# Strassen's seven products in place of eight for the down projection of an MLP, with weight sums by accumulating fetches and activation sums on GpSimd

## The chip, the cores and the metric

The kernel runs on one core of a Trainium2 chip. The metric is the device time of one execution in microseconds (us), lower is better. A core has TensorE (matmuls, PE in the profile; PEld is its weight load), VectorE (DVE), ScalarE (ACT), GpSimd (POOL) and SyncE (SP, which here only issues transfers). Matmul results land in the banks of PSUM; all other tiles lie in SBUF.

## The reference

The kernel computes one layer of a decoder trunk in fp32: three token mixers, their merge, and an MLP. The change touches the last product of the MLP alone, with x of 512 tokens x 1024 channels and 3072 hidden channels:

```python
h2 = rms_norm(x, norm_ffn[l])
up = causal_dwconv(h2 @ w_up[l], ffn_conv_w[l], ffn_conv_b[l])
gate_h, val_h = jnp.split(up, 2, axis=-1)
x = x + (jax.nn.gelu(gate_h, approximate=True) * val_h) @ w_down[l]
...
return rms_norm(x, final_norm)
```

## The kernel before, in words

**Products of three matmuls.** Every fp32 operand of a product is kept as a head and a rest. `split` (L94, L95) makes the head by a copy on ScalarE into the matmul's own type and the rest by a subtraction on VectorE. `mm3` (L101) then issues three matmuls for one product: head by head, head by rest, rest by head. All big matmuls have a 128x128 stationary and a 128x512 moving operand.

**Units.** The program is a list of units, each with a block of weights (512 KB), and of steps of other work between them. `emit` walks the list and calls `fetch` (L152: one load on SyncE's queue and the splits) for a unit two units ahead of it (`AHEAD`). The order in which each engine gets its instructions follows from that list and from a scheduler behind it.

**The MLP.** Hidden channels come in three groups of 1024 (eight tiles of 128). For a group, 16 up units run first: 24 matmuls each, one 128x512 result [hidden channel, token]. `up_evac` reads it with one ACT operation (L910) and two DVE operations (L912, the causal convolution). After each second unit `up_done` applies GELU on ScalarE, multiplies on VectorE (L923) and splits the product into head and rest, so that it can be the stationary operand of the down projection.

**The down projection** of a group adds [512 tokens, 1024 hidden] by [1024, 1024] weights to the residual `x2`: eight tiles [128 tokens, 512 channels] `x2[t][c]`, called `m` in the profile. `down_units` makes two rounds of four units, one round for each half c of the output channels. A unit of `token_units` holds 256 hidden rows of weights and has 24 matmuls, six into each of four PSUM banks (one for each 128 tokens t); behind the fourth unit the four banks are added to x2 by DVE (`evac`, L858). So a group has 8 x 24 = 192 matmuls. In the last group the second round is made by `token_held`: all four blocks of weights are held, and the tiles of tokens follow one another with 24 matmuls each, so that the final norm of one runs beside the matmuls of the next.

**The final norm** of 128 tokens: `evac` squares x2 with a sum along the rows (ACT, L121); `final` multiplies the second half by the gain on GpSimd (L951), takes the sum of both squares (L872), runs `rsqrt` (L109 to L115, twelve small DVE operations that each need the one before), scales the first half (`normed`, L877, DVE) and the second (L954, ACT), and stores both (L955, L956).

The name `raw` stands for weights as loaded, `whi` and `wlo` for head and rest of a block, `r` for heads and rests in smaller tiles, `f` for fp32 tiles, `mm` for PSUM banks, `st` for columns of row statistics.

## Time and profile before

| | |
|---|---|
| time, median of 3 runs | 954.41 us (954.19 to 954.55) |
| span of the profiled execution | 952.6 us, granted TensorE clock 0.997 |
| median less span | 1.8 us |
| TensorE busy | 940.8 us (99%), 4522 matmuls |
| VectorE, ScalarE, GpSimd busy | 572.4, 452.8, 11.1 us |
| the three groups of the MLP | from 559.54 us to the last matmul at 943.84 us |

One execution was recorded by the profiler. Its span runs from its first to its last instruction, and the runs' median is 1.8 us above it. In the views below, a row of the timeline has start, duration, engine, line, operation, the tile written and the tiles read, the shape, and in brackets the idle time before it and what ended that. Where a row stands for several instructions (x2, x3), its duration is from the first one's start to the last one's end. Neighbours in a row overlap a little, so the time that one more of them takes is the difference between rows of different counts.

### The profile page before, as it was taken

Reading aid. Unit: us, or ns where it says so; the run is one execution under the profiler, and the core shown is the slowest. Engines: PE = TensorE matmul, PEld = TensorE weight load, DVE = VectorE, ACT = ScalarE, POOL = GpSimd, SP = SyncE. Lnnn points to the kernel's source line nnn. Section 1 sums busy time; section 2 is a strip of 40 time slices with the busy share of each in tenths; the row PEclk is TensorE's granted clock in tenths of the full one; section 3 lists DMA queues with packets and bytes.
Section 4 is the critical chain, followed back from the end, with each engine's and each line's share of the span. In section 5 each row is a group of like instructions: output and inputs, shape, how many; then the busy total and the mean of one; then the engine's idle time right before and its main releaser. Section 6 shows DMA issues by size and latency. Waiting matters only on the chain.

```text
span 952.6 us, 11687 instructions
## 1 busy us (share of the span) xinstructions
PE 940.8 (99%) x4522; PEld 798.2 (84%) x4522; DVE 572.4 (60%) x1003; ACT 452.8 (48%) x682; POOL 11.1 (1%) x27
## 2 busy tenths in 40 slices
PE   8999999999999999999999999999999999999996
PEld 6899888887897789998888898888888888888885
DVE  7897754565744774485576756663456643556646
ACT  7565645684955783343334434442244432344432
POOL 0000000000000000000000000000000000000002
PEclk9999999999999999999999999999999999999998
DMA  7446212222232232222266202232232332322312
GB/s 231 152 138 193 67 57 68 80 92 78 75 117 79 77 99 84 78 94 72 67 197 224 77 23 88 89 105 95 90 109 89 97 102 90 107 93 91 131 45 88
DMA packets 30839, 95.95 MB, mean 101 GB/s; under 512 B 3568, under 2 KB 4736, under 8 KB 30784
## 3 DMA queue, kind: packets, MB, share of 16 engines
q1 hardware_dynamic: 30208, 94.16, 30.7%
q10 hardware_dynamic: 576, 1.05, 0.3%
q8 instruction: 35, 0.57, 0.2%
q14 instruction: 20, 0.16, 0.1%
HBM read 93.10 MB, written 2.10 MB: 100 GB/s over the span
## 4 chain that ended last, share of the span: by engine, by line
PE 95%; DVE 3%; DMA 0%; ACT 0%; issue 0%; SPq 0%; DVEq 0%; ACTq 0%
PE mm L101 89%; PE sm L101 3%; PE mm L328 1%; DVE wlo L95 1%; PE sm L787 1%; DMA m<-in_xT 0%; DVE r L95 0%; PE sm L789 0%; PE sm L773 0%; DVE m L296 0%; PE sm L760 0%; PE sm L895 0%; PE sm L808 0%; DVE hl L95 0%; PE sm L502 0%
## 5 line engine op out<-in xcount | busy, mean ns | idle before, releaser
L95 DVE TENSOR_TENSOR wlo<-raw,whi 128x1024 fp32r<-128x1024 f32 (+3 forms) x171 | 189.2, 1110 | 215.7 <-PE mm L101 98.6
L94 ACT ACTIVATE whi<-raw 128x1024 fp32r<-128x1024 f32 (+3 forms) x171 | 164.6, 966 | 198.1 <-PE mm L101 176.4
L101 PE MATMUL mm<-h2l,whi 128*128 128x512 f32 x360 | 140.1, 389 | 0.0
L101 PE MATMUL mm<-h2h,whi 128*128 128x512 f32 x360 | 139.9, 389 | 0.0
L101 PE MATMUL mm<-whi,r 128*128 128x512 f32 (+1 forms) x448 | 135.3, 381 | 0.0
L101 PE MATMUL mm<-hh,whi 128*128 128x512 f32 x288 | 113.9, 396 | 0.0
L101 PE MATMUL mm<-hl,whi 128*128 128x512 f32 x288 | 112.6, 391 | 0.0
L101 PE MATMUL mm<-r,whi 128*128 128x512 f32 (+1 forms) x448 | 98.3, 368 | 0.0
L101 PEld LDWEIGHTS mm<-whi,r 128*128 128x128 f32 x448 | 83.7, 188 | 15.0
L101 PEld LDWEIGHTS mm<-r,whi 128*128 128x128 f32 x448 | 77.9, 189 | 14.6 <-issue 0.8
L101 PE MATMUL mm<-h2h,wlo 128*128 128x512 f32 x360 | 88.9, 389 | 0.0
L101 PE MATMUL mm<-wlo,r 128*128 128x512 f32 (+1 forms) x224 | 85.6, 382 | 0.2 <-DVE wlo L95 0.2
L101 PEld LDWEIGHTS mm<-h2l,whi 128*128 128x128 f32 x360 | 67.6, 188 | 14.0
L101 PEld LDWEIGHTS mm<-h2h,wlo 128*128 128x128 f32 x360 | 67.6, 188 | 14.0
L101 PEld LDWEIGHTS mm<-h2h,whi 128*128 128x128 f32 x360 | 67.5, 188 | 13.9
L912 DVE SCALAR_TENSOR_TENSOR f<-mm,prm,f 128x511 f32<-128x511 f32 x96 | 71.7, 746 | 7.8 <-ACT f L910 6.1
L101 PE MATMUL mm<-hh,wlo 128*128 128x512 f32 x288 | 71.2, 389 | 0.0
L101 PEld LDWEIGHTS mm<-hh,whi 128*128 128x128 f32 x288 | 54.1, 188 | 11.6 <-issue 0.4
L101 PEld LDWEIGHTS mm<-hh,wlo 128*128 128x128 f32 x288 | 54.1, 188 | 11.2
L101 PEld LDWEIGHTS mm<-hl,whi 128*128 128x128 f32 x288 | 54.1, 188 | 10.7
L94 ACT ACTIVATE r<-f 128x512 fp32r<-128x512 f32 (+4 forms) x47 | 27.2, 589 | 65.0 <-DVE f L923 61.8
L101 PE MATMUL mm<-r,r 128*128 128x512 f32 (+1 forms) x240 | 56.8, 391 | 0.0
(191 smaller groups left out, 1208.0 us busy)
## 6 DMA issues: line engine op xcount, KB each, us to landing
raw<-in_wup SPq DMA_DIRECT2D x48, 512.0 KB, 3.5
raw<-in_wch SPq DMA_DIRECT2D x40, 512.0 KB, 3.3
raw<-in_wdown SPq DMA_DIRECT2D x24, 512.0 KB, 3.5
raw<-in_wbr SPq DMA_DIRECT2D x24, 384.0 KB, 3.1
raw<-in_wvg SPq DMA_DIRECT2D x12, 384.0 KB, 3.0
raw<-in_wout SPq DMA_DIRECT2D x8, 512.0 KB, 3.5
raw<-in_wmk SPq DMA_DIRECT2D x6, 512.0 KB, 3.4
raw<-in_wmv SPq DMA_DIRECT2D x8, 384.0 KB, 3.1
```

Of the source, the lines that this page charges most:

```text
L94: nc.scalar.activation(hi, src, AF.Copy)
L95: (eng or nc.vector).tensor_tensor(out=lo, in0=src, in1=hi.bitcast(F32), op=ALU.subtract)
L101: nc.tensor.matmul(ps, lhsT=l, rhs=r, start=first and i == 0, stop=last and i == len(seq) - 1)
L328: nc.tensor.matmul(ps[u], lhsT=a, rhs=b, start=q == 0 and i in (0, 2), stop=q == KD - 2 and i >= len(seq) - 2)
L787: nc.tensor.matmul(ps[:, j, :], lhsT=sT[h][:, t, :], rhs=vt[t][hp][:, j, :], start=True, stop=t == 0)
L912: nc.vector.scalar_tensor_tensor(out=a[:, j:], in0=ps[:, :S - j], scalar=col(C_FCW + 48 * (2 - j) + f), in1=a[:, j:], op0=ALU.mult, op1=AL ...
```

## The change

The product of a group is made from halves of both operands: the tokens in two halves of 256, the hidden channels in two halves (even and odd tiles), the output channels in two halves of 512. The plain way has eight products of such halves. The change uses seven, called a1, a2, c1, b1, c2, b2 and b3, on sums and differences of the halves (Strassen's scheme in Winograd's form). Each product has two parts p (four of the hidden tiles' pairs each half) of 12 matmuls, so a group has 14 units of 12 = 168 matmuls.

What goes with it:

- Weights. A product's weights are half tiles of 128x512. B11, B21, B22 and B12 are loaded plainly by SyncE's queue (L994). The sums of weights are made in place: a fetch from GpSimd's queue adds another quarter of the weights to what lies in SBUF (`accum_op`, L999): B11 + B12, then + B22, then + B21, and B12 + B22; sixteen transfers of 256 KB in a group. A group's transfers move 8 MB in place of 4. The tile that is added to is read by a split before. A product's weights are split in four half tiles (28 x 128x512 in a group, where there were 8 x 128x1024).
- Activations. The up stage no longer splits them. GpSimd makes the sums of halves (`sums` and `s4`, L1036 to L1048: 16 operations of 128x256 in a group), and each product's operand is split when its unit comes (14 times 512 columns in a group, where there were 8).
- Results. The banks come in pairs (two tiles of 128 tokens). The second product of a, c and b goes on into the bank of the first, which is read in between: a1, b1 and b2 are kept in SBUF tiles `e` over the groups (`keep`: a copy on ScalarE in the first group, L1055; an addition on VectorE in the others, L1057), the others are added to x2 (`put`, L1060).
- Last group. The kept sums are put where they belong: additions of `e` to x2 on VectorE (`fix`, L1063) and of one kept sum to another on GpSimd (L1084, L1094). Squares and the final norm follow: of the first two tiles of tokens behind c2, of the last two behind b3.
- Order. `emit` takes for each unit a list of (lead, function) pairs in place of the one fetch two units ahead: loads 5 to 9 units ahead, adding fetches 4 to 7, splits of weights 3, splits of activations 2 (a1: 1).

The scheme's core in the diff (comment lines that change in other places are left out):

```diff
+    def down_fast(g, at):
...
+        def load(q, p):
...
+                loads.append(nc.sync.dma_start(ts[j], wdown[g, int(q[1]) - 1, int(q[2]) - 1, p, :, j, :]))
+        def add(to, q, p):
+            for j in range(2):
+                nc.gpsimd.dma_start(raw[to, p][j], wdown[g, int(q[1]) - 1, int(q[2]) - 1, p, :, j, :],
+                                    accum_op=ALU.add)
+        def ready(key, q, p):
...
+            for j in range(2):
+                split(*ts[j], raw[q, p][j])
+            w[key, p] = ts
+        def act_ready(key, p):
...
+        def sums(p):
...
+            for j in range(2):
+                tt(out=s1[:, j, :], in0=A[2, 1, j], in1=A[2, 2, j], op=ALU.subtract)
+            for j in range(2):
+                tt(out=s2[:, j, :], in0=s1[:, j, :], in1=A[1, 1, j], op=ALU.subtract)
+            for j in range(2):
+                tt(out=A[2, 1, j], in0=A[1, 1, j], in1=A[2, 1, j], op=ALU.subtract)
...
+            def s4():
...
+                    tt(out=A[1, 1, j], in0=A[1, 2, j], in1=s2[:, j, :], op=ALU.add)
+        def keep(k, i, ps):
+            if g == 0:
+                e[k, i] = fslot()
+                nc.scalar.activation(e[k, i], ps, AF.Copy)
+            else:
+                nc.vector.tensor_tensor(out=e[k, i], in0=e[k, i], in1=ps, op=ALU.add)
...
+        def read(key, i, ps):
+            if key == "a1":
+                keep("a1", i, ps)
+                if lastg:
+                    fix(2 + i, 0, e["a1", i], ALU.add)
+            elif key == "a2":
+                put(i, 0, ps)
+                if lastg:
+                    square(i, 0)
+            elif key == "c1":
+                put(2 + i, 1, ps)
+            elif key == "b1":
+                keep("b1", i, ps)
+                if lastg:
+                    nc.gpsimd.tensor_tensor(out=e["b1", i], in0=e["b1", i], in1=e["a1", i], op=ALU.add)
+                    fix(i, 1, e["b1", i], ALU.subtract)
+            elif key == "c2":
+                put(i, 1, ps)
+                if lastg:
+                    square(i, 1)
+                    final(i)
+            elif key == "b2":
+                keep("b2", i, ps)
+                if lastg:
+                    nc.gpsimd.tensor_tensor(out=e["b2", i], in0=e["b2", i], in1=e["a1", i], op=ALU.add)
+                    fix(2 + i, 1, e["b2", i], ALU.subtract)
+                    square(2 + i, 1)
+            else:
+                put(2 + i, 0, ps)
+                if lastg:
+                    square(2 + i, 0)
+                    final(2 + i)
+        def run(key, p):
...
+            for i in range(2):
+                if key[1] == "1" and p == 0:
+                    banks[b, i] = bank()
+                tk = slice(i * P, (i + 1) * P)
+                mm3(banks[b, i], [(hi[:, j, tk], lo[:, j, tk], *ws[j]) for j in range(2)],
+                    key[1] == "1" and p == 0, p == 1, key[1] != "1")
+                if p == 1:
+                    read(key, i, banks[b, i])
+        pre = {
+            "a1": ("B11", [(6, lambda p: load("B11", p))]),
+            "a2": ("B21", [(6, lambda p: load("B21", p))]),
+            "c1": ("B11", [(6, lambda p: add("B11", "B12", p))]),
+            "b1": ("B11", [(4, lambda p: add("B11", "B22", p))]),
+            "c2": ("B22", [(5, lambda p: load("B22", p)), (4, lambda p: late[p]())]),
+            "b2": ("B12", [(9, lambda p: load("B12", p)), (7, lambda p: add("B12", "B22", p))]),
+            "b3": ("B11", [(6, lambda p: add("B11", "B21", p))]),
+        }
...
     for g in range(3):
-        acts = []
-        weave(up_units(g, acts, 3 if g == 0 else 0), [])
...
+        us, sums = down_fast(g, act)
+        up = up_units(g, act, 3 if g == 0 else 0)
+        weave(up[:8], [])
+        step(sums[0])
+        weave(up[8:], [])
+        step(sums[1])
         if g == 2:
             step(lambda: gain_rows(gfin))
-        weave(down_units(wdown[g], acts, final if g == 2 else None), [])
+        for u in us:
+            made_unit(*u)
```

Three places in the order of the instructions show what moved. The first is TensorE at the start of the second group's down projection. Before, a unit starts with a bank of its own and goes on to the next bank after six matmuls (`mm_1219`, `mm_1220`):

```order
L101 MATMUL mm_1219_6565<-whi_1205_6485,r_1130_6023 128x512
L101 MATMUL mm_1219_6565<-wlo_1206_6486,r_1130_6023 128x512
L101 MATMUL mm_1219_6565<-whi_1205_6485,r_1142_6099 128x512
L101 MATMUL mm_1219_6565<-wlo_1206_6486,r_1142_6099 128x512
L101 MATMUL mm_1219_6565<-whi_1205_6485,r_1131_6024 128x512
L101 MATMUL mm_1219_6565<-whi_1205_6485,r_1143_6100 128x512
L101 MATMUL mm_1220_6566<-whi_1205_6485,r_1130_6023 128x512
```

With the change, the end of a1 (banks `mm_1282`, `mm_1283`, weights `whi_1261`) and the start of a2 (weights `whi_1268`) stand here:

```order
L102 MATMUL mm_1283_6756<-wlo_1262_6639,r_1274_6729 128x512
L102 MATMUL mm_1283_6756<-whi_1261_6638,r_1275_6730 128x512 x2
L102 MATMUL mm_1282_6749<-whi_1268_6682,r_1276_6735 128x512
L102 MATMUL mm_1282_6749<-wlo_1269_6683,r_1276_6735 128x512
L102 MATMUL mm_1282_6749<-whi_1268_6682,r_1276_6735 128x512
L102 MATMUL mm_1282_6749<-wlo_1269_6683,r_1276_6735 128x512
L102 MATMUL mm_1282_6749<-whi_1268_6682,r_1277_6736 128x512 x2
L102 MATMUL mm_1282_6749<-r_1278_6741,r_1284_6763 128x512
L102 MATMUL mm_1282_6749<-r_1279_6742,r_1284_6763 128x512
```

The first bank that a2 writes is `mm_1282`, which a1 has just left: the reading of a1 from it, on VectorE, lies between the two, where before a bank was read only behind its round of four units. The rows that follow fill `mm_1282` with all 12 matmuls of a2 before `mm_1283` gets its own.

The second place is VectorE at the same time, from the last up unit on. Before, the convolution (L912), the product (L923) and the split of the last activation are followed by the weights of the next units and by the reading of the first round:

```order
L923 TENSOR_TENSOR f_1208_6514<-f_1208_6514,f_1213_6549 128x512
L95 TENSOR_TENSOR r_1215_6556<-f_1208_6514,r_1214_6555 128x512
L95 TENSOR_TENSOR wlo_1225_6596<-raw_1223_6593,whi_1224_6595 128x1024
L95 TENSOR_TENSOR wlo_1228_6626<-raw_1226_6623,whi_1227_6625 128x1024
L95 TENSOR_TENSOR wlo_1231_6656<-raw_1229_6653,whi_1230_6655 128x1024
L858 TENSOR_TENSOR m_894_4553<-m_894_4553,mm_1219_6565 128x512
L858 TENSOR_TENSOR m_895_4555<-m_895_4555,mm_1220_6566 128x512
```

With the change, behind the last product (L943) and one split of weights, the order is this (`r_1275`, `r_1277`, `r_1285` are rests of activations; `wlo_1295`, `r_1279`, `r_1281` and `r_1287` of weights; `f_1110` and `f_1111` are the kept sums of a1):

```order
L96 TENSOR_TENSOR r_1275_6730<-f_1224_6430,r_1274_6729 128x256
L96 TENSOR_TENSOR r_1275_6730<-f_1251_6587,r_1274_6729 128x256
L96 TENSOR_TENSOR wlo_1295_6800<-f_1243_6519,whi_1294_6799 128x512
L96 TENSOR_TENSOR r_1277_6736<-f_1189_6203,r_1276_6735 128x256
L96 TENSOR_TENSOR r_1277_6736<-f_1211_6349,r_1276_6735 128x256
L96 TENSOR_TENSOR r_1279_6742<-raw_1258_6604,r_1278_6741 128x512
L1057 TENSOR_TENSOR f_1110_5775<-f_1110_5775,mm_1282_6749 128x512
L96 TENSOR_TENSOR r_1281_6744<-raw_1258_6604,r_1280_6743 128x512
L96 TENSOR_TENSOR r_1285_6764<-f_1237_6507,r_1284_6763 128x256
L96 TENSOR_TENSOR r_1285_6764<-f_1264_6671,r_1284_6763 128x256
L96 TENSOR_TENSOR r_1287_6770<-f_1234_6478,r_1286_6769 128x512
L1057 TENSOR_TENSOR f_1111_5783<-f_1111_5783,mm_1283_6756 128x512
```

Behind the last up unit there are now splits of activations, half tiles of weights for three products ahead, and between them the two readings of a1's banks.

The third place is VectorE at the end of the last group. Before, one tile of tokens' final norm (`f_1398`) is followed by the reading of the last tile, and then by its own norm:

```order
L114 TENSOR_TENSOR st_1397_7679<-st_1397_7679,st_1396_7678 128x1
L115 SCALAR_TENSOR_TENSOR st_1395_7677<-st_1397_7679,st_1395_7677 128x1
L877 SCALAR_TENSOR_TENSOR f_1398_7692<-m_895_4555,st_1395_7677,gain_1344_7423 128x512
L858 TENSOR_TENSOR m_928_4713<-m_928_4713,mm_1399_7697 128x512
L872 SCALAR_TENSOR_TENSOR st_1402_7727<-st_1369_7560 128x1
L109 TENSOR_SCALAR st_1403_7729<-st_1402_7727 128x1
```

With the change, behind the two interleaved chains of `rsqrt` of the first two tiles of tokens (26 small rows, `normed` of the first, and the keeping of b2's first bank) this stands:

```order
L887 SCALAR_TENSOR_TENSOR f_1530_8088<-m_895_4555,st_1527_8073,gain_1450_7735 128x512
L1063 TENSOR_TENSOR m_928_4713<-m_928_4713,f_1166_6051 128x512
L96 TENSOR_TENSOR r_1532_8094<-f_1365_7209,r_1531_8093 128x256
L1057 TENSOR_TENSOR f_1167_6059<-f_1167_6059,mm_1504_7952 128x512
L96 TENSOR_TENSOR r_1532_8094<-f_1387_7355,r_1531_8093 128x256
L96 TENSOR_TENSOR r_1534_8100<-f_1418_7524,r_1533_8099 128x512
L1063 TENSOR_TENSOR m_929_4715<-m_929_4715,f_1167_6059 128x512
L96 TENSOR_TENSOR r_1536_8102<-f_1419_7525,r_1535_8101 128x512
L96 TENSOR_TENSOR r_1538_8120<-f_1413_7513,r_1537_8119 128x256
L96 TENSOR_TENSOR r_1538_8120<-f_1440_7677,r_1537_8119 128x256
L1060 TENSOR_TENSOR m_896_4557<-m_896_4557,mm_1503_7945 128x512
L1060 TENSOR_TENSOR m_897_4559<-m_897_4559,mm_1504_7952 128x512
```

The rows ahead of the two `put` (L1060) hold the splits that the last units of TensorE need (`r_1532` to `r_1538`); they stand behind `normed` of both tiles, the keeping of b2 and the fixes that follow from it.

129 lines of the change are left out of this document (106 added, 23 removed).

## The prediction

> **What bounds the kernel now.** I read the totals and the clock first, then the chain that ended last, then busy time by stretch in the MLP, then the timeline where up units pass into the down projection, and its end.
>
> ```profile
> PE 940.8 (99%) x4522; PEld 798.2 (84%) x4522; DVE 572.4 (60%) x1003; ACT 452.8 (48%) x682; POOL 11.1 (1%) x27
> core 0: 952.6 us, clock 0.997
> 559.54 384.30 PE mm L101 x1728
> 790.00:800.00 10.00, 10.00 (x46) 8.29 (x45) 3.82 (x4) 2.12 (x2) 0.00 (x0) 1.00 0.28 98
> 860.00:870.00 10.00, 10.00 (x45) 8.26 (x44) 5.81 (x8) 4.84 (x6) 0.00 (x0) 1.00 0.26 87
> ```
>
> TensorE is the bound: busy 99% at full clock. In the chain the whole MLP is one link, 1728 matmuls from 559.54 to 943.84 without a wait, 384.30/1728 = 0.2224 us each. The third and fourth rows are 10 us of a down projection and of up units (columns: TensorE, weight load, VectorE, ScalarE, GpSimd, clock, DMA): beside a full TensorE, VectorE is busy for 3.82 and 5.81, GpSimd for nothing. So matmuls taken away count in full as long as VectorE keeps up, and that is the question, since the change takes from TensorE and gives to VectorE.
>
> **What is removed.** 3 x (192 - 168) = 72 matmuls of unchanged shape: 72 x 0.2224 = **-16.0 us**. A unit of 12 is 2.67 us, a group's 14 units 37.4.
>
> **What VectorE gets, and the front of a group.** Prices from the passage into the last down projection (whose first matmul starts at 900.15, my zero):
>
> ```profile
> 900.15 0.39 PE L101 MATMUL mm<-whi,r 128*128 128x512 f32 x1
> 900.35 0.78 ACT L910 ACTIVATE f<-mm,prm 128x512 f32<-128x512 f32 x1 [0.75 <-PE mm L101]
> 901.55 1.53 DVE L912 SCALAR_TENSOR_TENSOR f<-mm,prm,f 128x511 f32<-128x511 f32 x2
> 904.38 1.66 ACT L94 ACTIVATE r<-raw 128x512 fp32r<-128x512 f32 x3
> 904.51 0.69 DVE L95 TENSOR_TENSOR r<-f,r 128x512 fp32r<-128x512 f32 x1 [0.70 <-ACT r L94]
> 905.12 1.89 DVE L95 TENSOR_TENSOR r<-raw,r 128x512 fp32r<-128x512 f32 x3
> 906.89 0.61 ACT L94 ACTIVATE r<-raw 128x512 fp32r<-128x512 f32 x1
> ...
> 9.80 0.75 DVE L95 TENSOR_TENSOR wlo<-raw,whi 128x256 fp32r<-128x256 f32 x2
> L95 DVE TENSOR_TENSOR wlo<-raw,whi 128x256 fp32r<-128x256 f32 x8 | 3.1, 418 | 0.2 <-ACT whi L94 0.2
> 810.11 1.28 DVE L858 TENSOR_TENSOR m<-m,mm 128x512 f32<-128x512 f32 x2
> ```
>
> A split or sum of 512 columns costs VectorE (1.89 - 0.69)/2 = 0.60, one of 256 0.75 - 0.42 = 0.33, the reading of a bank 1.28 - 0.69 = 0.59; a head of 512 costs ScalarE (1.66 - 0.61)/2 = 0.52. At the front ScalarE reads the last up bank until 0.98; VectorE follows with 1.53 and the product, 0.60, and is free at 3.1. Then come, by the order above, two weight rests, four half-width ones, a third weight rest and the first `keep`: 3.1 + 3 x 0.60 + 4 x 0.33 + 0.60 = 6.8. a2's first matmul writes that bank, and TensorE reaches it at 5.34: 1.5 us lost in the second group, and 0.25 the same way from b2 to b3, where VectorE is nearly even: 1.75. In the first group `keep` stands on ScalarE: 3.1, then four half-width heads (taken as 0.31 each, little over half of 0.52), three of 512 and the copy, 3.1 + 1.24 + 1.56 + 0.52 = 6.4: 1.1 lost.
>
> **The end of the last group.** From 3.1 to the last split (`r_1538`) VectorE has, by the order, 44 operations of 512 columns, 18 of 256, two `normed` and 26 small ones. The chain behind the last matmul prices the rest:
>
> ```profile
> 931.84 0.75 DVE L877 SCALAR_TENSOR_TENSOR f<-m,st,gain 128x512 f32<-128x512 f32 x1
> 943.87 0.69 DVE L858 TENSOR_TENSOR m<-m,mm 128x512 f32<-128x512 f32 x1 [0.46 <-PE mm L101]
> 944.59 0.63 ACT L121 ACTIVATE junk<-m 128x512 bf16<-128x512 f32 x1 [1.15 <-DVE m L858]
> 945.35 0.63 DVE L872 SCALAR_TENSOR_TENSOR st<-st 128x1 f32<-128x1 f32 x1 [0.79 <-ACT junk L121]
> 946.01 0.15 DVE L109 TENSOR_SCALAR st<-st 128x1 int32<-128x1 int32 x1
> ...
> 947.94 0.16 DVE L115 SCALAR_TENSOR_TENSOR st<-st,st 128x1 f32<-128x1 f32 x1
> 948.13 0.75 DVE L877 SCALAR_TENSOR_TENSOR f<-m,st,gain 128x512 f32<-128x512 f32 x1
> ```
>
> Small ones 0.16 (0.19 where each waits for the one before: 946.01 to 947.94 is ten steps), `normed` some 0.67 in a row: 3.1 + 26.4 + 5.9 + 1.3 + 4.2 = 40.9 if VectorE never waits. Eight matmuls are left then (1.8): 42.7 against 37.4, **5.3 lost at least**, this group's front among it. VectorE will wait as well: four `fix` stand two or three rows behind a `keep`, with a GpSimd addition of 1.29 (rows below) between them, 0.7 each; 0.2 for a square; 26 x 0.03 for chained steps, 0.8. Together 3.8, so the group loses 5.3 to 9.1; I take 9.1, since the order is fixed and VectorE can't run past a wait. TensorE stands before b3 meanwhile: its activations' rests are queued behind both `normed` and the keeping of b2.
>
> Behind the last matmul, 943.84 to 952.6 is 8.8 now. With the change two norms end together: six small steps (0 to 1.0) and one more `normed` (0.67) stand ahead: 0.7 to 2.5 if the stores also queue; taken as **1.6**, all of the first two.
>
> **GpSimd against VectorE.** No row has half-width sums on GpSimd; a full one is quoted, half of it is 0.65. What speaks against the change is what small VectorE operations do beside it:
>
> ```profile
> 928.38 1.29 POOL L951 TENSOR_TENSOR f<-m,gain 128x512 f32<-128x512 f32 x1 [578.93 <-DVE m L858]
> 929.09 0.59 DVE L872 SCALAR_TENSOR_TENSOR st<-st 128x1 f32<-128x1 f32 x1 [0.85 <-ACT junk L121]
> 933.82 1.30 POOL L951 TENSOR_TENSOR f<-m,gain 128x512 f32<-128x512 f32 x1 [4.16 <-DVE m L858]
> 934.47 0.67 DVE L872 SCALAR_TENSOR_TENSOR st<-st 128x1 f32<-128x1 f32 x1 [0.79 <-ACT junk L121]
> L872 DVE SCALAR_TENSOR_TENSOR st<-st x8: 158/377/667, 533.9 to 945.3; 128x1 f32<-128x1 f32 x8
> ```
>
> L872 takes 0.16 at best; beside L951 it takes 0.59 and 0.67, and ends within 0.02 us of GpSimd's end (929.67 and 929.68; 935.12 and 935.14). It reads two columns of SBUF, and is held until GpSimd is done. The Trainium skill ("SBUF — State Buffer", Who interferes with whom) calls it an exclusive lock: a VectorE instruction with two SBUF inputs and a GpSimd one that reads SBUF shut each other out for the whole instruction; by that rule the full price below would count, an estimate of 968.7 us for the kernel, and the row agrees.
>
> Splits, fixes and products have two SBUF inputs. Five half-width sums fall behind the last product in each front (three of the last tiles, two of `s4`): 5 x 0.65 = 3.2, three times 9.7. At the end four more additions and gain products matter: half of each of the four additions (0.65) and both gain products of the first two tiles (1.29): 2.6 + 2.6 = 5.2. Full price 14.9, none 0. About 15 of 21 VectorE rows in a front read SBUF twice, so I take 0.7 of it: **10.4**.
>
> **The clock.**
>
> ```profile
> 944.00:948.00 4.00, 0.00 (x0) 0.00 (x0) 2.86 (x14) 0.72 (x2) 1.26 (x1) 0.81 0.35 131
> 948.00:952.60 4.60, 0.00 (x0) 0.00 (x0) 0.85 (x2) 0.72 (x1) 0.00 (x0) 0.50 0.30 114
> ```
>
> After the last matmul the granted clock (second last but one) averages 0.81 over 4 us and is 0.50 after that: it fell about 2.5 us into the idle time. TensorE's stand before b3 is longer, so its last matmuls may run at half speed: 0 to 24 of them, 0 to 5.3; those behind the last split count, 8 x 0.2224 = **1.8**. The Trainium skill ("TensorE: Matmul & The Clock Gate", Part 1) has the half clock after an idle window of some 3.4 us and the full one after as much work, so all 24 would be slow, an estimate of 5.3; the drop agrees, the way back no row here shows.
>
> **Loads.** Bytes double only in the down stages, 8 MB to 37 us and the six units ahead of them, under the 231 GB/s that the first slice moved:
>
> ```profile
> GB/s 231 152 138 193 67 57 68 80 92 78 75 117 79 77 99 84 78 94 72 67 197 224 77 23 88 89 105 95 90 109 89 97 102 90 107 93 91 131 45 88
> m<-in_xT SPq DMA_DIRECT2D x8, 256.0 KB, 4.7
> m<-in_x SPq DMA_DIRECT2D x8, 256.0 KB, 3.0
> ```
>
> So I price bytes at 0. SyncE's plain loads stand 5 to 9 units ahead, 13 us or more against 3.0 to 4.7 to land: 0. An adding fetch has no row: at 256 KB it lies between 3.0 and 9.4 (twice 4.7, for reading what it adds to). The tightest, B22 onto B11, can start when c1's first split is done (8.7 by the same count) and is needed by b1's first unit at 6 x 2.67 + 1.75 = 17.8; two heads and two rests take 2 x (0.52 + 0.60) = 2.2 of the 9.1 between, hand-overs perhaps 0.6: 6.3 of slack. I take it as covered. Queued in order behind its wait on GpSimd are the last `s4` sums, wanted by c2 only at 21.4: 0.
>
> **Sum.** -16.0 + 1.1 + 1.75 + 9.1 + 1.6 + 10.4 + 1.8 = +9.8. From the span, 952.6 + 9.8 = 962.4; the median lies 1.8 above the span: **964.2 us**. Its own bounds: VectorE lock at 0.4 instead of 0.7 and no clock drop give 958; full lock, 5.3 at half clock and a tail of 2.5 give 973. A difference under 0.2% (1.9 us) counts as none.
>
> **Rivals.**
>
> *Faster: GpSimd doesn't hold VectorE where it matters.* Losses are then 1.1 + 1.75 + 5.3 to 9.1 + 1.6 = 9.8 to 13.6, without the clock: 948.2 to 952.0. For it: by the stretches VectorE idles 42 to 62% of the MLP, and many GpSimd sums may fall into that; a held sum only shifts an operation that had slack. Against: the two pairs above, and a down stage in which VectorE has some 41 us of work in 37. It decides if all losses stay under 14.1. Chance 0.21.
>
> *No difference.* With half the lock at the fronts alone (under 5 us), or no lock and the clock drop (953.8). Chance 0.09.
>
> *Slower by another mechanism: the adding fetches land late.* At 9.4 the tightest fetch comes 3.1 late in each of three groups, TensorE waits in front of b1: 9.3 on top of the sum, 973.5; with half of that 969. For it: four times the transfers on one queue behind waits on splits. Against: 6.3 of slack. Chance 0.15.
>
> *The change doesn't do what it says:* the order shows 168 matmuls a group, all of 128x512, so this is out.
>
> **Chances.** Forecast 0.55 and late fetches 0.15 make slower 0.70; same 0.09; faster 0.21. The range leaves out the lower part of the faster case (below 950) and full late fetches with full lock: 950 to 976.
>
> **What would show it.** Right: 72 matmuls fewer; TensorE waiting for VectorE (`keep`, line 1057, or a copy, 1055) behind a1, 1 to 3 us a group, more with the sums; splits of 512 columns that take over 0.9 us while GpSimd runs sums; one wait of 5 us or more ahead of b3 in the last group, followed by a granted clock under 1; 10 us behind the last matmul. Wrong: splits of 0.60 beside GpSimd sums (no lock); waits of TensorE on GpSimd's queue or its transfers at b1 (late fetches); a wait ahead of b3 under 3 us (VectorE ran ahead).

## The result, and the profile after

The changed kernel takes 980.57 us (median of 4 runs, 979.43 to 980.81) against 954.45 (median of 4): a ratio of 1.0272, 95% interval 1.0257 to 1.0286. It is slower, as forecast, but by 26.1 us where 9.8 were forecast, outside the range of 950 to 976.

The totals of the changed kernel's page and its span:

```profile
PE 938.2 (96%) x4450; PEld 789.6 (81%) x4450; DVE 632.1 (65%) x1125; ACT 488.8 (50%) x792; POOL 98.8 (10%) x127
core 0: 977.7 us, clock 0.987
```

The 72 matmuls are gone (4522 to 4450), and TensorE is still busy for 938 us: what was won stands there as waits and as matmuls at a lower clock. Where, the first matmul of each down stage and the last of the kernel tell:

```profile
639.40 0.39 PE L102 MATMUL mm<-whi,r 128*128 128x512 f32 x1
...
776.00 0.39 PE L102 MATMUL mm<-whi,r 128*128 128x512 f32 x1
...
912.09 0.39 PE L102 MATMUL mm<-whi,r 128*128 128x512 f32 x1
...
966.71 1.54 PE L102 MATMUL mm<-r,r 128*128 128x512 f32 x6
```

Before, these starts are 639.03, 769.59 and 900.15, and the last matmul ends at 943.83:

```profile
639.03 0.39 PE L101 MATMUL mm<-whi,r 128*128 128x512 f32 x1
...
769.59 0.39 PE L101 MATMUL mm<-whi,r 128*128 128x512 f32 x1
```

An up stage takes 87.04 us (682.55 to 769.59 before). So the three down stages took 43.5, 43.5 and 43.7 us before, and take 49.6, 49.1 and 56.2 now; 168 matmuls without a wait are 168 x 0.2267 = 38.1. The losses are 11.5, 11.0 and 18.1 us, where the forecast had 3.4, 4.0 and 16.8 (front, the group's part of holding, and for the last one the clock). **The last group's sum came near the forecast; the first two lost some three times as much.**

What TensorE waited for (us in all, times, the longest):

```profile
PE mm L102 <- ACT r L95: 17.2, 6, 7.2
PE mm L102 <- DVE f L1057: 7.1, 4, 3.1
PE mm L102 <- DVE r L96: 3.0, 4, 0.9
```

The second row is waits for a `keep`: a1's in the second and third groups (1.9, 3.1 and 0.6 us, in a2) and b2's ahead of b3 in the second (1.5). The first row is heads of activations on ScalarE, which is busy for half of the span. Its two long ones are 7.2 us ahead of b3 in the last group and 5.8 us ahead of c1's second unit in the first.

Each front (the first units of a down stage) begins with two short waits inside a1, for the head and the rest of its own second half: 1.03 and 0.69 us in the first group, 1.02 and 0.69 in the others. ScalarE's row and TensorE's two of the first group:

```profile
642.31 0.63 ACT L95 ACTIVATE whi<-f 128x512 fp32r<-128x512 f32 x1 [1.94 <-PE mm L102]
...
643.30 0.50 PE L102 MATMUL mm<-whi,r 128*128 128x512 f32 x1 [1.03 <-ACT r L95]
...
645.19 1.67 PE L102 MATMUL mm<-whi,r 128*128 128x512 f32 x3 [0.69 <-DVE r L96]
```

In ScalarE's queue a head of weights stands ahead of a1's second half, and it waits 1.94 us until TensorE ends the first half: TensorE waits for an engine that waits for it. The forecast had neither of these waits.

The wait of 5.8 us in the first group has this behind it (the chain, and then ScalarE's own rows):

```profile
652.27 0.60 POOL f L999
652.86 8.89 DMA f<-in_wdown
662.32 0.62 ACT r L95
...
660.18 0.63 ACT L95 ACTIVATE whi<-f 128x512 fp32r<-128x512 f32 x1 [10.04 <-DMA f<-in_wdown]
661.78 0.63 ACT L95 ACTIVATE whi<-f 128x512 fp32r<-128x512 f32 x1 [0.97 <-DMA f<-in_wdown]
```

ScalarE sits for 10 us on the heads of b1's weights, whose two adding fetches are issued from 652.27 on; the second takes 8.9 us to land, at 661.75. The activations of c1's second unit stand behind the first of these heads in ScalarE's queue. What SyncE issues just ahead of these fetches, and GpSimd's issue of them:

```profile
651.10 1.93 SPq L994 DMA_DIRECT2D f<-in_wdown  x4
...
652.27 1.75 POOL L999 DMA_DIRECT2D f<-in_wdown  x2 [2.58 <-DVE r L96]
```

The issue comes 12.9 us into the stage, where 8.7 was forecast: GpSimd is idle for 2.58 us ahead of it and waits for c1's split on VectorE. And the fetches aren't alone: SyncE's four plain loads of 256 KB (B12) are issued from 651.10 on and land between 657.19 and 661.13, 6.1 to 8.5 us after their issues. Why c1's split is late, VectorE's and GpSimd's rows of the same front show:

```profile
643.58 0.68 DVE L96 TENSOR_TENSOR wlo<-f,whi 128x512 fp32r<-128x512 f32 x1
644.18 1.82 DVE L96 TENSOR_TENSOR r<-f,r 128x256 fp32r<-128x256 f32 x2
645.93 1.22 DVE L96 TENSOR_TENSOR wlo<-f,whi 128x512 fp32r<-128x512 f32 x1
647.07 2.42 DVE L96 TENSOR_TENSOR r<-f,r 128x256 fp32r<-128x256 f32 x2
...
643.74 1.11 POOL L1036 TENSOR_TENSOR f<-f,f 128x256 f32<-128x256 f32 x1 [1.65 <-DVE f L943]
644.93 0.80 POOL L1038 TENSOR_TENSOR f<-f,f 128x256 f32<-128x256 f32 x1
645.68 0.91 POOL L1040 TENSOR_TENSOR f<-f 128x256 f32<-128x256 f32 x1
647.15 1.71 POOL L1048 TENSOR_TENSOR f<-f,f 128x256 f32<-128x256 f32 x2
```

Two half-width rests take 1.82 and 2.42 us where a row of the kernel before has 0.75, a full one 1.22 where it had 0.68, as long as GpSimd makes its five sums. And the granted clock (third column from the end) falls to half behind waits: twice in the first group, twice in the second, and in the last only behind the stand ahead of b3. Here the first front, and a row of the last group behind the same two waits inside a1, where the clock stayed at 1.00:

```profile
644.00:646.00 2.00, 1.31 (x5) 0.36 (x3) 2.00 (x4) 2.00 (x7) 1.92 (x3) 0.87 0.13 47
646.00:648.00 2.00, 2.00 (x6) 1.57 (x6) 2.00 (x3) 1.86 (x5) 2.00 (x4) 0.50 0.00 0
...
658.00:660.00 2.00, 0.00 (x0) 0.00 (x0) 0.00 (x0) 0.00 (x0) 1.47 (x2) 1.00 1.12 235
...
662.00:664.00 2.00, 1.02 (x2) 0.83 (x3) 1.56 (x3) 2.00 (x5) 2.00 (x4) 0.63 0.94 152
664.00:666.00 2.00, 2.00 (x6) 1.61 (x5) 2.00 (x4) 2.00 (x5) 1.36 (x2) 0.51 1.02 165
...
918.00:920.00 2.00, 1.85 (x7) 1.22 (x8) 2.00 (x3) 2.00 (x6) 2.00 (x4) 1.00 0.98 347
```

In the second row TensorE is busy for all of 2 us and gets through six records where ten stand at full clock. The DMA share (second last) is at about 1 through the long wait (1.12, and 0.94 at its end), while TensorE, VectorE and ScalarE stand: the wait lasts as long as the transfers do. In the last group the stand ahead of b3 is there, and half clock behind it:

```profile
952.00:954.00 2.00, 0.00 (x0) 0.00 (x0) 1.90 (x12) 0.20 (x2) 1.37 (x2) 1.00 0.00 0
954.00:956.00 2.00, 0.00 (x0) 0.00 (x0) 2.00 (x14) 0.72 (x1) 0.00 (x0) 1.00 0.00 0
956.00:958.00 2.00, 0.00 (x0) 0.00 (x0) 1.90 (x5) 0.00 (x0) 1.26 (x1) 0.52 0.69 259
958.00:960.00 2.00, 0.88 (x2) 0.79 (x3) 2.00 (x4) 1.83 (x4) 0.00 (x0) 0.50 0.24 86
960.00:962.00 2.00, 2.00 (x6) 1.52 (x6) 2.00 (x3) 1.87 (x6) 1.66 (x2) 0.50 0.50 187
```

VectorE is full throughout, with the small steps of the two norms (12 and 14 records), as the prediction had it.

### The profile page after: what moved, and what is told of

Its sections match the earlier page's. It is cut to its first block, busy times and chain, and to the rows that moved or that the text cites. A ratio compares the mean times of both kernels' runs of the same rounds, so it can differ in the third digit from the quotient of the medians.

```text
span 977.7 us, 12013 instructions
## 1 busy us (share of the span) xinstructions
PE 938.2 (96%) x4450; PEld 789.6 (81%) x4450; DVE 632.1 (65%) x1125; ACT 488.8 (50%) x792; POOL 98.8 (10%) x127
## 4 chain that ended last, share of the span: by engine, by line
PE 83%; DVE 7%; DMA 4%; issue 2%; ACT 1%; POOL 1%; SPq 0%; ACTq 0%; POOLq 0%; DVEq 0%
PE mm L102 77%; DMA f<-in_wdown 4%; PE sm L102 3%; DVE r L96 2%; DVE wlo L96 2%; PE mm L338 1%; ACT r L95 1%; POOL f L999 1%; PE sm L797 1%; DMA m<-in_xT 0%; POOL f L1048 0%; PE sm L799 0%; PE sm L783 0%; DVE m L306 0%; PE sm L770 0%
## 5 line engine op out<-in xcount | busy, mean ns | idle before, releaser
L96 DVE TENSOR_TENSOR wlo<-raw,whi 128x1024 fp32r<-128x1024 f32 (+4 forms) x157 | 171.4, 1097 | 187.7 <-PE mm L102 99.2
L95 ACT ACTIVATE whi<-raw 128x1024 fp32r<-128x1024 f32 (+4 forms) x157 | 147.2, 943 | 195.3 <-PE mm L102 173.8
L102 PE MATMUL mm<-whi,r 128*128 128x512 f32 (+1 forms) x344 | 112.9, 400 | 26.5 <-ACT r L95 17.2
L102 PEld LDWEIGHTS mm<-whi,r 128*128 128x128 f32 x344 | 66.9, 196 | 45.2 <-ACT r L95 19.7
L102 PE MATMUL mm<-r,r 128*128 128x512 f32 (+1 forms) x324 | 79.4, 396 | 1.0 <-DVE r L96 0.9
L102 PEld LDWEIGHTS mm<-r,r 128*128 128x128 f32 (+1 forms) x324 | 60.1, 186 | 15.8 <-DVE r L96 1.7
L102 PE MATMUL mm<-wlo,r 128*128 128x512 f32 (+1 forms) x172 | 67.8, 394 | 0.2 <-DVE wlo L96 0.2
L96 DVE TENSOR_TENSOR r<-f,r 128x256 fp32r<-128x256 f32 (+4 forms) x107 | 64.9, 639 | 1.7 <-ACT r L95 1.6
```

What stands on the lines that cost most here:

```text
L95: nc.scalar.activation(hi, src, AF.Copy)
L96: (eng or nc.vector).tensor_tensor(out=lo, in0=src, in1=hi.bitcast(F32), op=ALU.subtract)
L102: nc.tensor.matmul(ps, lhsT=l, rhs=r, start=first and i == 0, stop=last and i == len(seq) - 1, skip_group_check=more)
```

## The experiments

The theory from these views: a front is a chain in series. GpSimd's sums hold VectorE, so c1's weights are split late; the adding fetch waits for that split and is slow itself; b1 waits for it; and the clock falls on top. Rivals were ScalarE's queue order, the place of the fetches in GpSimd's queue, and the mere amount of VectorE's work. Every run below is compared with runs of the kernel before on the same chip (954.4 to 954.7); stage lengths are taken as above, and the tail is the time from the end of the last matmul to the end of the span.

| run | us | ratio, 95% interval | three down stages, us | tail, us |
|---|---|---|---|---|
| before | 954.45 | | 43.5, 43.5, 43.7 | 8.8 |
| changed | 980.57 | 1.0272 (1.0257 to 1.0286) | 49.6, 49.1, 56.2 | 9.5 |
| c1's activations first | 982.25 | 1.0289 (1.0274 to 1.0304) | 48.0, 50.0, 61.2 | 9.3 |
| fetches that don't add | 973.44 | 1.0200 (1.0184 to 1.0215) | 46.4, 46.7, 55.6 | 9.5 |
| no activation sums | 967.27 | 1.0136 (1.0119 to 1.0152) | 44.4, 44.8, 52.8 | 9.0 |
| both left out | 961.41 | 1.0077 (1.0062 to 1.0092) | 42.6, 45.5, 51.2 | 8.9 |
| norms late | 980.10 | 1.0270 (1.0255 to 1.0286) | 51.3, 50.8, 51.3 | 13.3 |
| own tile for b1 | 975.42 | 1.0216 (1.0201 to 1.0231) | 48.0, 46.0, 58.5 | 9.2 |
| memsets for sums | 965.81 | 1.0113 (1.0096 to 1.0129) | 43.3, 45.8, 53.4 | 9.1 |
| sums that nobody uses | 977.63 | 1.0239 (1.0223 to 1.0254) | 48.7, 51.0, 56.5 | 9.1 |
| sums on VectorE | 978.73 | 1.0248 (1.0233 to 1.0264) | 47.3, 46.8, 61.3 | 9.1 |
| idle matmuls | 975.29 | 1.0219 (1.0205 to 1.0233) | 48.3, 48.2, 54.6 | 9.3 |
| last group plain | 967.04 | 1.0133 (1.0118 to 1.0148) | 49.8, 49.6, 43.7 | 8.9 |
| plain, own tile, VectorE | 958.96 | 1.0046 (1.0030 to 1.0062) | 45.4, 43.3, 43.7 | 8.8 |
| reordered | 950.44 | 0.9960 (0.9948 to 0.9973) | 42.3, 42.4, 43.7 | 8.8 |
| second order | 947.50 | 0.9926 (0.9914 to 0.9939) | 39.9, 40.1, 43.7 | 8.8 |
| second order, GpSimd | 955.27 | 1.0009 (1.0000 to 1.0018) | 46.0, 41.8, 43.7 | 8.8 |
| second order, all groups | 953.33 | 0.9990 (0.9981 to 1.0000) | 40.1, 40.2, 45.2 | 13.5 |

The stages are those of one profiled execution, and it can lie some us from the median: 3.6 above it with sums that nobody uses, 2.4 above it with both left out, 3.0 below it for "plain, own tile, VectorE". So single stages are read to about 2 us.

**Is it ScalarE's queue?** c1's activations go ahead of the waiting head:

```diff
-                            (1 if key == "a1" else 2, lambda key=key, p=p: act_ready(key, p))],
+                            ({"a1": 1, "c1": 4}.get(key, 2), lambda key=key, p=p: act_ready(key, p))],
```

> Edit: c1's activations are split four units ahead instead of two, so that on ScalarE they stand ahead of the heads of b1's weights, which wait for the adding fetch. Queue theory (a late adding fetch holds ScalarE's queue, and c1's last unit, though its own data are there, waits behind it): one unit of 12 matmuls, 2.7 us, moves ahead of the wait in each group, 5 to 8 us in all, so 972 to 976 us; the wait of 5.8 us in the first group shrinks to about 3 and stands at b1. Lock theory (GpSimd's sums slow VectorE): within 1 us of 980.6.

It took 982.25, and neither expectation was met. In the first group the wait of 5.8 us is gone and none stands at b1. But the splits that moved ahead are VectorE's work too, and TensorE now waits for a rest in a2:

```profile
652.27 2.08 PE L102 MATMUL mm<-r,r 128*128 128x512 f32 x4 [4.45 <-DVE r L96]
```

The first group gained 1.6 us; the last lost 5, with a wait of 11.1 us ahead of b3 in place of 7.2. So ScalarE's queue passes the lateness on, and its order alone gives nothing: VectorE is behind, and with it the fetch, which is issued 13.5 us into the stage here.

**What does the adding cost?**

```diff
-                nc.gpsimd.dma_start(raw[to, p][j], wdown[g, int(q[1]) - 1, int(q[2]) - 1, p, :, j, :],
-                                    accum_op=ALU.add)
+                nc.gpsimd.dma_start(raw[to, p][j], wdown[g, int(q[1]) - 1, int(q[2]) - 1, p, :, j, :])
```

> Edit: the fetches from GpSimd's queue no longer add, they overwrite the tile (the sums of weights are left out). Queue, waits and bytes stay the same. Fetch theory: an adding fetch of 256 KB is slow in itself (8 to 10 us to land at the fronts, 2.9 for a plain one), so each of the three groups gets 4 to 6 us shorter: 963 to 969 us. Rival, issue theory (the time lies in GpSimd's queue, in what stands ahead of the fetch and in making it): 977 to 981 us. Lock theory: 979 to 981 us.

973.44: 7.1 us less, 3.2 and 2.3 of it in the first two groups, between the two expectations. The same transfers (kind, packets, MB, share of 16 engines' time in 40 us; median landing over the run), first as changed, then without adding:

```profile
q0 software_dynamic: 1728, 3.15, 46.9%
...
f<-in_wdown POOLq DMA_DIRECT2D x48, 256.0 KB, 5.5
```

```profile
q0 software_dynamic: 960, 3.15, 23.1%
...
f<-in_wdown POOLq DMA_DIRECT2D x48, 256.0 KB, 3.4
```

Adding keeps the transfer engines busy for twice as long (46.9% against 23.1% for the same bytes) and lands 2.1 us later at the median. At b1 of the first front the two plain fetches take 6.1 and 6.5 us, the two adding ones 7.9 and 8.9: most of the landing time is there without adding. SyncE's four loads run beside both; no run moves them away, so what they cost the fetch stays open.

**Do the sums on GpSimd hurt, and both together?** The sums are left out, the products take plain halves; then without adding too:

```diff
...
-            for j in range(2):
-                tt(out=s1[:, j, :], in0=A[2, 1, j], in1=A[2, 2, j], op=ALU.subtract)
...
-                         ("c1", p): s1, ("b1", p): s2,
+                         ("c1", p): [A[2, 2, j] for j in range(2)], ("b1", p): [A[2, 1, j] for j in range(2)],
...
```

> Edit: GpSimd's sums of activations are left out, the products take plain halves in place of the sums. The fetches stay. Lock theory: VectorE's splits at the fronts go from 0.9 to 1.2 us back to 0.6, each group gets 2 to 3.3 us shorter: 971 to 975 us. Fetch theory: the wait for b1's weights stays, and what VectorE wins is spent waiting in front of it: 977 to 980 us.

> Edit: both at once, the fetches from GpSimd's queue overwrite instead of adding (sums of weights left out) and GpSimd's sums of activations are left out. Chain theory (in a front, VectorE's splits, held by GpSimd's sums, come first, then the adding fetch that waits for them, then b1: two delays in series): the two savings add up, 13.3 + 7.1 = 20 us off 980.6, 959 to 962 us, and down stages of 40 to 42 us in the first two groups. Rival (either one alone is what is waited for last): not much below the 967.3 us without the sums alone, 965 to 967.

967.27 without the sums: 13.3 us, more than either theory gave. Without both 961.41: 19.2 us, near the sum of the two (20.4). Had one of the two delays hidden the other, the second would have given little. The link between them shows in the issue of b1's fetch: 12.9 us into the first stage as changed, 9.0 without the sums.

**Holding, or waiting for the sums?** Three runs change what GpSimd does: memsets in the sums' places (two for each sum, one for each of `s4`), the same sums into scratch tiles, and the sums on VectorE.

```diff
...
+            for k in range(3):
+                for j in range(2):
+                    nc.gpsimd.memset((s1, s2)[k % 2][:, j, :], 0.0)
+                    nc.gpsimd.memset((s1, s2)[k % 2][:, j, :], 0.0)
...
```

```diff
-                tt(out=A[2, 1, j], in0=A[1, 1, j], in1=A[2, 1, j], op=ALU.subtract)
+                tt(out=s1[:, j, :], in0=A[1, 1, j], in1=A[2, 1, j], op=ALU.subtract)
...
-                         ("c1", p): s1, ("b1", p): s2,
+                         ("c1", p): [A[2, 2, j] for j in range(2)], ("b1", p): [A[2, 1, j] for j in range(2)],
...
```

```diff
-            tt = nc.gpsimd.tensor_tensor
+            tt = nc.vector.tensor_tensor
...
```

> Edit: GpSimd's sums of activations are left out, and in the place of each stand two memsets of the same size, so that GpSimd is busy at the same place in its queue but reads nothing from SBUF. Lock theory (what hurts is that both engines read two inputs from SBUF): as without the sums, 966 to 969 us. Queue theory (what hurts is that the fetches stand behind the sums in GpSimd's queue): 974 us or more.

> Edit: as changed, GpSimd makes the same sums from the same halves at the same places, but they go to scratch tiles that no product uses (the products take plain halves). So GpSimd reads SBUF beside VectorE as in the changed kernel, and nothing waits for a sum. Lock theory: the 13.3 us that leaving the sums out gave are the holding of VectorE, and come back: 976 us or more. Rival, order theory (without the sums, products have their operands sooner and the order of VectorE's work is another; holding costs little): 965 to 969 us as with memsets.

> Edit, a version that computes all of it: as changed, only the sums of activations are made by VectorE in place of GpSimd (the few additions and gain products of the last group stay on GpSimd). Lock theory: the holding of VectorE's splits goes (13.3 us with the sums left out), and 16 sums of 0.33 us are added, of which 5 to 7 a group stand in the front: 969 to 973 us. Work theory (VectorE's amount of work is the bound of the down stage): 979 us or more.

965.81 with memsets, 977.63 with sums that nobody uses. VectorE's rows of the same first front, with memsets:

```profile
643.40 1.28 DVE L96 TENSOR_TENSOR wlo<-f,whi 128x512 fp32r<-128x512 f32 x2
644.60 1.42 DVE L96 TENSOR_TENSOR r<-f,r 128x256 fp32r<-128x256 f32 x4
645.94 1.29 DVE L96 TENSOR_TENSOR r<-raw,r 128x512 fp32r<-128x512 f32 x2
```

and with unused sums:

```profile
643.66 0.68 DVE L96 TENSOR_TENSOR wlo<-f,whi 128x512 fp32r<-128x512 f32 x1
644.26 1.84 DVE L96 TENSOR_TENSOR r<-f,r 128x256 fp32r<-128x256 f32 x2
646.03 1.22 DVE L96 TENSOR_TENSOR wlo<-f,whi 128x512 fp32r<-128x512 f32 x1
647.17 2.38 DVE L96 TENSOR_TENSOR r<-f,r 128x256 fp32r<-128x256 f32 x2
649.48 1.82 DVE L96 TENSOR_TENSOR r<-raw,r 128x512 fp32r<-128x512 f32 x2
```

The same two full and four half-width rests take 2.6 us in the one (643.40 to 646.02) and 5.9 in the other (643.66 to 649.55): 3.3 us of holding in a front, with no product waiting for a sum. The memsets are a weaker comparison than was meant: they wait for no product, and most of them run before these rows. Two stand beside VectorE's rows:

```profile
645.51 1.18 POOL L1044 MEMSET f<- 128x256 f32 x2
```

The two full rests at 645.94 take 1.29 beside them, and two take 1.28 where GpSimd runs no sum (649.41 as changed). GpSimd's queue isn't what makes b1's fetch late: with unused sums GpSimd idles for 2.7 us ahead of the issue and waits for VectorE, as in the changed kernel, and the issue comes 12.8 us into the stage; with memsets it comes at 9.0. So it is the reading of SBUF by both engines, and neither GpSimd's queue nor the wait for a sum. The Trainium skill ("SBUF — State Buffer", Who interferes with whom) names both halves of this: two SBUF inputs on VectorE against a GpSimd instruction that reads SBUF exclude each other, one that only writes does not; the rows agree with both (5.9 against 2.6 us with sums, 1.29 beside memsets).

The sums on VectorE took 978.73, above the 969 to 973 of the lock theory and just under the work theory's 979. The first two groups gained 2.3 each; the last, where VectorE is full, lost 5.1, with a wait of 12.4 ahead of b3. Taking work off GpSimd onto a full VectorE gives back most of what the holding cost.

**Can the chain be cut?** b1's sum is made in a tile of its own, early:

```diff
-            "b1": ("B11", [(4, lambda p: add("B11", "B22", p))]),
+            "b1": ("Y", [(12, lambda p: load("Y", p, "B11")), (11, lambda p: add("Y", "B12", p)), (10, lambda p: add("Y", "B22", p))]),
...
```

> Edit, a version that computes all of it: b1's and b3's sum of weights is made in a tile of its own, loaded and added to twice during the up stage (B11 loaded once more, B12 added once more), so that no fetch waits for c1's splits ahead of b1. GpSimd's sums stay as they are. Chain theory: the wait for b1's weights goes in all groups, 4 to 6 us each: 962 to 969 us. Rival, load theory (adding fetches are slow because they load the transfer engines, and 12 more in a group make the others later): 979 us or more.

975.42, 5.2 us less: 1.6 and 3.0 in the first two groups of the profiled execution, while its last group is 2.3 longer. The fetch is off the path in these two, and what is late next takes most of the place: TensorE waits for a1's `keep` (5.1 us in two waits of VectorE's line, one of 3.4 for ScalarE's copy) and for the heads of activations. Neither expectation was met; the load theory's 979 is out.

**What does the clock cost?** Matmuls whose results nobody uses, where TensorE stood:

```diff
+            n = {("a1", 1): (8, 8, 8), ("a2", 0): (0, 8, 12), ("c1", 1): (24, 4, 0), ("b3", 0): (0, 4, 32)}.get((key, p))
+            if n and n[g]:
+                ps = sbank()
+                for k in range(n[g]):
+                    nc.tensor.matmul(ps, lhsT=kept[0], rhs=kept[1], start=k == 0, stop=k == n[g] - 1)
...
```

> Edit: matmuls that nobody uses (8 to 32 of 128x512, 1.8 to 7.2 us) stand where TensorE waits in the changed kernel: ahead of a1's second half, of a2 or of c1's second half, and of b3 in the last group. Nothing else changes. Clock theory (the short waits bring the granted clock down, and the half clock behind them costs some 8 us by the windows): the clock stays near 1 and 4 to 7 us go: 974 to 977 us. Rival (matmuls behind a wait are waiting for VectorE's next split anyway, the clock costs nothing): 980 us or more.

```profile
core 0: 974.0 us, clock 0.997
```

975.29 with 108 matmuls more, and the clock is back at 0.997 (0.987 as changed). By this run the half clock costs 5.3 us, and more matmuls make this kernel faster.

**The last group.** Norms issued behind everything; the last group with eight products; and (below) the new order in all groups:

```diff
                 if lastg:
                     square(i, 1)
-                    final(i)
...
```

```diff
-        lastg = g == NF // 8 - 1
+        lastg = False
...
+            weave(plain_up(g, old), [lambda i=i, k=k: late_fix(k, i) for k in range(5) for i in range(2)])
...
+            weave(down_units(wd, Tiles(old), final), [])
```

> Edit: in the last group all four final norms are issued behind the last product, so the splits of b3 stand ahead of the two chains of small operations on VectorE. Order theory (b3 waits because VectorE's order puts both chains first): the wait of 6 us or more ahead of b3 and the half clock behind it go, 6 to 9 us, of which 1 to 3 come back as a longer tail: 973 to 976 us. Rival, work theory (VectorE has too much to do in that group, in whatever order): 979 to 982 us.

> Edit, a version that computes all of it: the last group is made as before the change, with eight products, and the kept sums of the first two groups are put in place by VectorE during its up stage. First two groups as changed. If the groups' losses are their own: the last group's 56.2 us become 43.7 and the tail 8.8: 980.6 - 12.5 - 0.7 = 967 to 968 us. If the first groups' late work is only pushed along to where it ends: 972 us or more.

Late norms: 980.10. The last stage got 4.9 us shorter, the tail 3.8 longer, with 1.7 more in each of the first two groups, which the edit doesn't touch. That is the work theory's 979 to 982: in another order the same work is late in another place. With a plain last group 967.04, as expected: 13.5 us less, and the other two groups as in the changed kernel.

**Versions that compute all of it.** The plain last group with b1's own tile and the sums on VectorE; then the parts of the products in another order, on six banks (shown as in the second order):

```diff
-                    banks[b, i] = bank()
+                    banks[b, i] = sbank() if (b, i) == ("b", 1) else bank()
...
+        seq = [(k, 0) for k in ("a1", "c1", "b1")] + [(k, 1) for k in ("a1", "c1", "b1")]
+        seq += [(k, p) for k in ("a2", "b2", "c2", "b3") for p in range(2)]
+        for key, p in seq:
...
```

> Edit, a version that computes all of it: last group with eight products (as in the run with a plain last group), the tile of its own for b1's weights, and the sums of activations on VectorE in place of GpSimd. Lock and chain theory: in the first two groups only the waits for the last activations and for keeping a1 stay, 3 to 4.5 us over the 38.1 of 168 matmuls, 41 to 43 us against 43.5 before: 949.5 to 953.5 us. Rival, work theory (VectorE has no room for 16 more sums in a group): groups of 45 us and more, 957 us or more.

> Edit, on top of the former: the parts of the products are reordered (a1 and c1 of the first half of the hidden tiles, then of the second, b1, a2, b2, c2, b3), with a sixth bank, so that no product writes the bank that was read just before and the last activations are needed 2.7 us later. If the rest of a front's loss is a1's keeping and the last activations: 38.5 to 40.5 us a group, 944.5 to 949 us, faster than before the change. Rival (VectorE is behind by the amount of its work, whatever the order): as the former run, 950 us or more.

> Edit, a version that computes all of it: last group with eight products, own tile for b1's weights, sums on VectorE, and the order a1, c1, b1 of the first half of the hidden tiles, then a1, c1, b1 of the second, then a2, b2, c2, b3, on six banks. The last activations are needed 8 us into the stage in place of 2.7, and between a bank's reading and its next use lie other products. Front theory (what is left of the loss is the waits of the front and the half clock behind them): 39 to 40.5 us a group, 946 to 949 us. Work theory (VectorE has more than a stage's time of work in it): 42 us and more a group, 951 us or more.

> Edit: the former version with the sums on GpSimd again. Lock theory: holding costs VectorE 2 to 5 us in each of two groups where it is full, so 3 to 8 us above the former version. Rival (with the order changed there is room, holding falls into idle time): within 2 us of the former version, or below it, since VectorE has 16 sums less in a group.

> Edit, a version that computes all of it: own tile, sums on VectorE and the new order of the fastest version, but seven products in the last group too, with its fixes and final norms. Work theory for the last group (VectorE has 41 us of work up to the last split in a stage of 38, whatever the order, and two norms end together): 50 to 56 us there against 43.7 with eight products, 954 to 961 us. Order theory (the last group lost its time by the same front as the others): 42 to 45 us there, 945 to 949 us.

Without a new order 958.96, 5 us over the expectation and on the side of its rival: a1's `keep` and the last activations stand in the front still. The first reordering gave 950.44, again just on the rival's side (in it the fetch for c1 adds to B11's tile ahead of a1's split, so a1 is made from B11 + B12; the amount of work is the same). The second one, with that mended, gave **947.50, a ratio of 0.9926 (0.9914 to 0.9939): 7 us faster than the kernel before.** Its down stages:

```profile
639.19 0.39 PE L102 MATMUL mm<-whi,r 128*128 128x512 f32 x1
...
766.14 0.39 PE L102 MATMUL mm<-whi,r 128*128 128x512 f32 x1
...
893.30 0.39 PE L102 MATMUL mm<-whi,r 128*128 128x512 f32 x1
...
PE mm L102 <- DVE r L96: 1.6, 2, 0.8
```

39.9 and 40.1 us, 2 above the bare matmuls, and 1.6 us of waits for rests in all. The same version with the sums on GpSimd takes 955.27: holding, with the waits and the lower clock that it brings (0.994 against 0.996), costs 7.8 us there, and all of the gain. With seven products in the last group too, 953.33, just under the slower expectation: that stage is 45.2 us (56.2 as changed) but the tail 13.5 (9.5). Together they are 11.8 us over 38.1 and 8.8, where the changed kernel has 18.8: 7 us were front, order and clock, and 11.8 are left for the group's own fixes and norms and for the sums, which VectorE makes there too. Eight products stay better there.

## Why the prediction was wrong

- **72 matmuls less:** right in number. Priced 16.0 by 0.2224 from a chain link that has shorter matmuls of the first group in it; at 0.2267 (5.44 for 24) they are 16.3.
- **GpSimd holds VectorE:** right in kind and size. 3.2 us a front was the full price, 3.3 are shown; the 0.7 that was taken of it was not needed. For the whole kernel 10.4 was taken; leaving the sums out gives 13.3, with all that follows from the holding.
- **"I take it as covered":** the failed step. The adding fetch was given 6.3 us to land, from an issue at 8.7 into the stage and a need at 17.8, and priced at 0. But 8.7 was counted without the holding that the part before it prices (without the sums the issue does come at 9.0), and from a VectorE free at 3.1, where it is free at 4.2. As changed, the issue comes at 12.9 and the landings at 20.8 and 22.4. And b1 was not the first to need them: c1's second unit, ahead of it, stands behind b1's heads in ScalarE's queue. Holding and fetch were treated as if they lay beside each other. They stand in series, on one chain from VectorE over the fetch back to TensorE: both left out give 19.2 us, nearly the sum of 13.3 and 7.1. In place of 0 the adding alone costs 7.1.
- **The fetch's own price** was bounded at 3.0 to 9.4 us; 8.9 was seen at the front of the first group, 5.5 is the median. "So I price bytes at 0" failed as well: the transfer engines were at a share of about 1 during the wait, since adding takes them twice as long per byte and four plain loads run beside it.
- **a1's second half:** a term put at nothing without a reason. The front was counted as if a1 ran through to 5.34; TensorE waits 1.0 and 0.7 us inside it in each group, 5.1 us in all.
- **The clock:** 1.8 us, in the last group alone. It falls in the first two groups as well; 5.3 us in all by the run with idle matmuls. The part's other estimate, all 24 matmuls of b3 slow, doesn't follow from the way back that it quotes: some eight matmuls at half speed fill that time, and the row 962:964 has the clock at 0.77 again, 1.00 behind it. The drop behind the last matmul, called agreeing, came 2.5 us into the idle time, sooner than the window that the part quotes.
- **a1's `keep`:** right in the second group, 1.9 us for 1.5. In the first group, where 1.1 was priced, TensorE doesn't wait for the copy; b2's, priced at 0.25, is 1.5. With the last group's (3.1 and 0.6) the waits for L1057 are 7.1 us in all.
- **The last group:** 16.8 us forecast, 18.1 measured, with the stand of 7 us ahead of b3. The share of the end's own work was about right, 9.1 + 1.6 with the tail, against 11.8 in the new order, where VectorE has the sums as well. Leaving the sums out takes 3.4 us off this stage, where 5.9 were priced as holding, and waits of 5.4 us stand in its front: that the total came out near is in part luck.
- **The tail:** 1.6 forecast, 0.7 measured.
- **The rivals:** the late fetches (chance 0.15, 969 to 973.5 us) were no rival of the holding, they came with it. The range names "full late fetches with full lock" and leaves it out; by the prediction's own figures that case is 973.5 + 4.5 = 978.0, the nearest of all to the 980.6 measured.
- **What the sum missed:** 16.4 us, from 964.2 to 980.6. By single runs the adding fetch gives 7.1, the clock 3.5 and the holding 2.9 more than forecast, 13.5 together. Each of these runs shifts the clock too, so no exact split is shown.

## What to carry to other kernels

When a change adds a wait on engine A and a delay to engine B, look first whether B's work is what A waits for: delays in series add up, and a slack is counted from the late time, not from the undisturbed one. Short waits of TensorE can also cost the clock behind them: here 1.0 and 0.7 us close together did in two of three groups. A product that gets cheaper on the bound engine is paid for on the others: it paid here only when the sums went off GpSimd, b1's sum of weights off the chain, the last group kept its eight products, and the order gave each bank's reading and the last activations time.

## What the runs showed of the hardware

- A fetch that adds into SBUF takes the transfer engines twice the time of a plain one per byte (46.9% against 23.1% of 40 us for 3.15 MB) and 5.5 against 3.4 us to land at the median; GpSimd spends 0.86 us issuing one, 0.54 for a plain one. With four plain loads of SyncE beside them, plain ones took 6.1 and 6.5 us, adding ones 7.9 and 8.9.
- GpSimd's sums of two SBUF tiles beside VectorE's subtractions lengthen both (half-width sums 0.74 us alone, up to 1.26 beside; two half-width rests 0.75 alone, 1.82 and 2.42 beside). Two memsets on GpSimd did not (two full rests took 1.29 beside them, 1.28 without).
- The granted clock fell to 0.50 behind waits of TensorE of 1.0 and 0.7 us that began 2.2 us apart, with no long wait before it, in the first two groups; behind the same two waits in the last group it stayed at 1.00. What decides isn't shown.
